# Moving the split weights and the transposed tokens of a hybrid decoder kernel by 16 and 32 bytes in SBUF

## The chip, the cores and the metric

The kernel runs on one core of a Trainium2 chip. The metric is the device time of one execution in microseconds (us); the kernel before takes 1882.4 us, the median of three runs (1880.84 to 1884.98).

## The reference

Two residual layers over 256 tokens of width 1024, and a final norm. Each layer has an attention mixer and then a product-key expert mixer (PEER). All of it is float32.

```
for i in range(2):
    h = rms_norm(x, attn_norm[i])
    x = x + (even_mixer if i == 0 else mla_mixer)(h, ...)      # projections, attention, out-projection
    h = rms_norm(x, ffn_norm[i])
    x = x + peer_ffn(h, w_q, sub_keys, u_tab, v_tab)
return rms_norm(x, final_norm)

# peer_ffn: q = h @ w_q; two top-16 lists of 128 keys for each of 8 heads; the best 16 of their sums name
# 16 of 16384 experts for each token and head; act = gelu(u_tab[expert] . h); out = sum softmax * act * v_tab[expert]
```

## The kernel before

The PEER mixer takes most of the time. The kernel doesn't gather experts. It multiplies all 256 tokens with the whole table `u` (16384 x 1024), multiplies the activations with a gate that is zero for every expert a token did not choose, and multiplies the result with the whole table `v`. Both tables stream through SBUF in units of 128 x 1024 float32 (512 KB), one DMA each on the sync queue, into three buffers `raw`.

TensorE takes its operands in fp32r, a rounded form of float32. To keep float32 precision each operand is split in two: `hi` is the rounded value and `lo` the rest. A product is then three matmuls: hi by hi, lo by hi, hi by lo. The class `Weights` (L46 on) splits each half unit of 512 columns: ScalarE writes `hi` from `raw` (L69), VectorE writes `lo` = raw - hi (L70). `hi` and `lo` have five buffers each (pools `hip` and `lop`). What the tokens need is split by `to_T` (L283 on): TensorE transposes a chunk of 128 features of all 256 tokens, ScalarE writes `hi[c]` (L290), VectorE `lo[c]` (L291). There are eight such chunks; `tiles8` (L281) reserves them.

A matmul has a *stationary* operand, 128 x 128, that a LDWEIGHTS puts into the array ahead of it, and a *moving* operand that is streamed through. The stages use the two kinds of tile in both roles:

- **projections** (`product`, L301 to L303) and **out-projection** (L438 to L440): tokens or head outputs stationary, split weights moving, 512 columns (352 and 200 in some).
- **PEER query and scores** ("the S stage", `split_prod`, L806 to L808): split weights stationary, tokens moving, 256 columns. One layer has 16 query blocks (tiles `rhi`, `rlo`) and 128 expert blocks (tiles `hi`, `lo`), 24 matmuls each. While the expert blocks run, the gates are made: groups of mostly eight bf16 matmuls (L990) stand between the S matmuls. In the query blocks and the first expert blocks VectorE also makes the top-16 lists (L831 to L838).
- **PEER output** ("the V stage", `mm`, L1078 to L1080): the split activations `ohA`, `ohB` stationary, the split weights moving, 512 columns, 1536 matmuls a layer.

Which byte of a partition an operand starts at is decided by its pool alone, which lays its tiles one behind another. Before, a `hi` or `lo` buffer of the weights is 2048 bytes a partition and a token tile is 1024 bytes, so all buffers of a kind start at the same place modulo 512 bytes.

Of the kernel before, what the change touches and what calls it, by code (L numbers as in the profile page):

```python
# [10 lines left out]
F32R = mybir.dt.float32r  # L11
# [9 lines left out]
S, D = 256, 1024  # L21
# [17 lines left out]
class Weights:  # L39
# [19 lines left out]
    def split(self, j):  # L59
        while self.n_split <= min(j, len(self.halves) - 1):  # L60
            k, s = self.halves[self.n_split]
            self.load(k + self.ahead)
            w = self.units[k][1]
            hi = self.hip.tile([128, 512], F32R, name="hi")
            self.tc_hp = self.tc.high_priority(offset=HP)
            self.tc_hp.__enter__()
            lo = self.lop.tile([128, 512], F32R, name="lo")
            src = self.raw[k][:, s * w:(s + 1) * w]
            self.nc.scalar.activation(hi[:, :w], src, AF.Copy)  # L69
            self.nc.vector.tensor_tensor(lo[:, :w], src, hi[:, :w].bitcast(F32), op=OP.subtract)  # L70
            self.tc_hp.__exit__(None, None, None)
            self.parts[self.n_split] = (hi, lo)
            self.n_split += 1
# [70 lines left out]
def body(tc, I, out):  # L144
    nc = tc.nc
    with ExitStack() as ctx:
# [132 lines left out]
            return x[tb][c // 4][:, c % 4 * 128:(c % 4 + 1) * 128]  # L279

        def tiles8(pool, name, dtype=F32R):  # L281
            return [pool.tile([128, S], dtype, name=f"{name}{c}") for c in range(8)]

        def to_T(src, c, col, hi, lo, psp, tag):

# [221 lines left out]
        def even_mixer(gcol):  # L507
            with ExitStack() as c1:
# [8 lines left out]
                va = ap.tile([128, 2, 64], F32, name="va")  # L517
                iw = ap.tile([128, 2, 8], F32, name="iw")
                oT = [tiles8(ap, f"oT{i}") for i in range(2)]
                selm = [ap.tile([128, 128 * (q + 1)], BF, name=f"selm{q}") for q in range(2)]  # L520
                hi, lo = tiles8(ap, "hi"), tiles8(ap, "lo")
                st = {}

# [104 lines left out]
        def mla_mixer(gcol):  # L628
            with ExitStack() as c1:
# [5 lines left out]
                cq = ap.tile([128, 2, D], F32, name="cq")  # L635
                scr = ap.tile([128, 2, D], F32, name="scr0")
                hi, lo = tiles8(ap, "hi"), tiles8(ap, "lo")
                chi, clo = tiles8(ap, "chi"), tiles8(ap, "clo")
                oT = [hi, lo]
# [520 lines left out]
```

## Time and profile before

| | |
|---|---|
| time, median of three runs | 1882.4 us |
| the profiled execution: its time, its span | 1880.96 us, 1879.2 us |
| busy: TensorE matmul, weight load, VectorE, ScalarE | 99%, 89%, 77%, 66% |
| chain of work that ended last, by engine | TensorE 92%, VectorE 6%, ScalarE 1%, issue 1% |
| the S stage's share of that chain (L806 to L808) | 39% |
| the V stage's share (L1078 to L1080) | 36% |

The span is the time from the first instruction to the last on the core; what lies around it is 1.8 us here. "Busy" of a matmul counts its streaming and its tail, so that two matmuls in a row overlap in the profile: how fast TensorE goes is read from the distance between starts, not from one matmul's duration. [...]

### The profile page before, as it was taken

To read this page: it belongs to the slowest core of one execution; us is meant where nothing else is said; L and a number is where in the kernel's file an instruction comes from. 1 tells how busy PE (TensorE), PEld (TensorE's weight loads), DVE (VectorE), ACT (ScalarE), POOL (GpSimd) and SP (SyncE) were. 2 spreads that over 40 slices of the span, in tenths; PEclk is the share of its full clock that TensorE was granted. 3 is DMA by queue.
4 is the path that set the end of the run, shared out by engine and by line. 5 is a ranking of instruction groups with operands and counts; after the bars stand their busy time and mean duration, and the time that the engine had idled before them with its cause. 6 is when DMAs were issued, how large, how long until landed. Compare 5 with 4: busy or idle time off the path is not lost.

```text
span 1879.2 us, 35739 instructions
## 1 busy us (share of the span) xinstructions
PE 1852.2 (99%) x12588; PEld 1664.2 (89%) x12588; DVE 1447.2 (77%) x3710; ACT 1247.3 (66%) x3060; POOL 6.4 (0%) x10
## 2 busy tenths in 40 slices
PE   8999999999999999999999999999999999999997
PEld 7769999999999888888888799999999988888886
DVE  7958998888898666666677699988888976666665
ACT  5646556888887555555576665688888865555554
POOL 0000000000000000000000000000000000000001
PEclk9989999999999999999999999999999999999999
DMA  6415565555555555556554345655555555555554
GB/s 191 134 46 170 163 197 182 168 169 174 165 170 179 191 193 193 191 193 192 188 162 136 122 139 190 190 174 165 172 167 169 171 189 191 192 192 193 192 193 136
DMA packets 90179, 323.33 MB, mean 172 GB/s; under 512 B 10512, under 2 KB 10896, under 8 KB 89744
## 3 DMA queue, kind: packets, MB, share of 16 engines
q1 hardware_dynamic: 88704, 318.71, 52.6%
q8 instruction: 99, 1.62, 0.3%
q0 software_dynamic: 288, 2.10, 0.3%
q14 instruction: 80, 0.66, 0.1%
q10 hardware_dynamic: 1008, 0.25, 0.1%
HBM read 319.97 MB, written 1.05 MB: 171 GB/s over the span
## 4 chain that ended last, share of the span: by engine, by line
PE 92%; DVE 6%; ACT 1%; issue 1%; DMA 0%; ACTq 0%; DVEq 0%
PE S L806 13%; PE S L807 13%; PE S L808 13%; PE acc L1079 12%; PE acc L1080 12%; PE acc L1078 12%; PE scp L990 3%; PE pj L301 2%; PE pj L303 2%; PE pj L302 2%; DVE lo L70 2%; PE bk L372 1%; DVE A L834 1%; DVE A L831 1%; DVE A L838 1%; PE pj L438 1%
## 5 line engine op out<-in xcount | busy, mean ns | idle before, releaser
L69 ACT ACTIVATE hi<-raw 128x512 fp32r<-128x512 f32 (+2 forms) x1214 | 756.0, 628 | 566.6 <-DVE lo L70 198.0
L70 DVE TENSOR_TENSOR lo<-raw,hi 128x512 fp32r<-128x512 f32 (+2 forms) x1214 | 826.2, 685 | 351.4 <-ACT hi L69 344.8
L806 PE MATMUL S<-hi,hi 128*128 128x256 f32 x2048 | 579.3, 283 | 1.8 <-ACT A L1019 1.8
L808 PE MATMUL S<-hi,lo 128*128 128x256 f32 x2048 | 568.9, 278 | 0.4
L807 PE MATMUL S<-lo,hi 128*128 128x256 f32 x2048 | 568.7, 278 | 0.0
L806 PEld LDWEIGHTS S<-hi,hi 128*128 128x128 f32 x2048 | 386.0, 188 | 2.6 <-ACT A L1019 2.6
L808 PEld LDWEIGHTS S<-hi,lo 128*128 128x128 f32 x2048 | 384.7, 188 | 1.2 <-DVE lo L70 1.1
L807 PEld LDWEIGHTS S<-lo,hi 128*128 128x128 f32 x2048 | 385.4, 188 | 0.0
L1079 PE MATMUL acc<-lo,ohB 128*128 128x512 f32 x512 | 201.2, 393 | 0.0
L1079 PE MATMUL acc<-lo,ohA 128*128 128x512 f32 x512 | 201.2, 393 | 0.0
L1080 PE MATMUL acc<-hi,ohA 128*128 128x512 f32 x512 | 199.9, 391 | 0.0
L1080 PE MATMUL acc<-hi,ohB 128*128 128x512 f32 x512 | 199.2, 391 | 0.0
L1078 PE MATMUL acc<-hi,ohA 128*128 128x512 f32 x512 | 159.2, 390 | 0.0
L1078 PE MATMUL acc<-hi,ohB 128*128 128x512 f32 x512 | 159.2, 390 | 0.0
L955 ACT ACTIVATE ohB<-ohB,RA 128x128 bf16<-128x128 bf16 x256 | 117.2, 525 | 0.0
L1078 PEld LDWEIGHTS acc<-hi,ohA 128*128 128x128 f32 x512 | 96.1, 188 | 22.0
L1078 PEld LDWEIGHTS acc<-hi,ohB 128*128 128x128 f32 x512 | 96.1, 188 | 21.9
L1079 PEld LDWEIGHTS acc<-lo,ohA 128*128 128x128 f32 x512 | 96.2, 188 | 20.8
L1079 PEld LDWEIGHTS acc<-lo,ohB 128*128 128x128 f32 x512 | 96.2, 188 | 20.7
L1080 PEld LDWEIGHTS acc<-hi,ohB 128*128 128x128 f32 x512 | 96.2, 188 | 20.3
L1080 PEld LDWEIGHTS acc<-hi,ohA 128*128 128x128 f32 x512 | 96.2, 188 | 20.3
L957 ACT ACTIVATE ohB<-iota,RA 128x128 bf16<-128x128 f32 x256 | 84.1, 435 | 0.0
(263 smaller groups left out, 2465.8 us busy)
## 6 DMA issues: line engine op xcount, KB each, us to landing
raw<-in_pu SPq DMA_DIRECT2D x256, 512.0 KB, 3.6
raw<-in_pv SPq DMA_DIRECT2D x256, 512.0 KB, 4.3
raw<-in_pq SPq DMA_DIRECT2D x32, 512.0 KB, 3.6
raw<-in_w SPq DMA_DIRECT2D x20, 512.0 KB, 3.7
raw<-in_uq SPq DMA_DIRECT2D x9, 512.0 KB, 4.0
raw<-in_w SPq DMA_DIRECT2D x12, 352.0 KB, 2.9
raw<-in_w0o SPq DMA_DIRECT2D x8, 512.0 KB, 3.6
raw<-in_w1o SPq DMA_DIRECT2D x8, 512.0 KB, 3.9
```

The costliest lines, as they stand in the source:

```text
L69: self.nc.scalar.activation(hi[:, :w], src, AF.Copy)
L70: self.nc.vector.tensor_tensor(lo[:, :w], src, hi[:, :w].bitcast(F32), op=OP.subtract)
L301: nc.tensor.matmul(ps[tb], hi[c][:, t], a, start=st, stop=False)
L806: nc.tensor.matmul(p, a, hi[c], start=first and i == 0, stop=False)
L807: nc.tensor.matmul(p, a, lo[c], start=False, stop=False)
L808: nc.tensor.matmul(p, b, hi[c], start=False, stop=last and i == 3)
L955: nc.scalar.activation(e[:, j // 2, :, j % 2], e[:, j // 2, :, j % 2], AF.Relu, bias=r[1], scale=r[2])
L957: nc.scalar.activation(e[:, j // 2, :, j % 2], iota, AF.Square, bias=r[0], scale=-1.0)
L990: nc.tensor.matmul(p[:, i], E[:, 1, i // 2, :, i % 2], G[:, s, i // 2, :, i % 2], start=i + s == 0, stop=True, skip_group_check=True)
L1078: nc.tensor.matmul(o, a[:, 0, t], w[0], start=b == 0, stop=False)
L1079: nc.tensor.matmul(o, a[:, 0, t], w[1], start=False, stop=False)
L1080: nc.tensor.matmul(o, a[:, 1, t], w[0], start=False, stop=b == NK - 1)
```

## The change

Three allocations change. A weight buffer is allocated with 520 columns and used with 512 (2080 bytes in place of 2048). A token tile is allocated with 264 columns and used with 256 (1056 bytes in place of 1024), and chunks 1, 3, 5, 7 start 4 columns (16 bytes) into their place. `tiles8` also reserves the head outputs `oT` of the first layer and the four sets of token tiles of each mixer.

```diff
-            hi = self.hip.tile([128, 512], F32R, name="hi")
+            hi = self.hip.tile([128, 520], F32R, name="hi")[:, :512]
...
-            lo = self.lop.tile([128, 512], F32R, name="lo")
+            lo = self.lop.tile([128, 520], F32R, name="lo")[:, :512]
...
         def tiles8(pool, name, dtype=F32R):
-            return [pool.tile([128, S], dtype, name=f"{name}{c}") for c in range(8)]
+            return [pool.tile([128, S + 8], dtype, name=f"{name}{c}")[:, 4 * (c % 2):4 * (c % 2) + S] for c in range(8)]
```

Every engine has the same instructions in the same order with the same waits in both programs; only addresses differ. The places of the operands in a partition, in bytes modulo 128 (the built programs' addresses; the buffers from first to last):

| operand | before | after |
|---|---|---|
| weights `hi`, five buffers | 96 96 96 96 96 | 96 0 32 64 96 |
| weights `lo`, five buffers | 96 96 96 96 96 | 0 32 64 96 0 |
| S stage: token tiles `hi` 0 to 7, and `lo` 0 to 7 | 32 (all) | 96 16 32 80 96 16 32 80 |
| V stage: `ohA`, `ohB` | 32 (all) | 96 (all) |
| first layer: token tiles of the projections, head outputs | 96 (all) | change like those of the S stage |
| `raw` | 96 (all) | 96 (all) |

The slices used within these tiles start at multiples of 512 bytes, except in the two projections with 200 and 352 columns.

## Rows read from the trace of the kernel before

**Rows 1.** The page: chain that ended last, by engine and by line.
```profile
PE 92%; DVE 6%; ACT 1%; issue 1%; DMA 0%; ACTq 0%; DVEq 0%
```

**Rows 2.** Busy time by stretch: us, then each engine's, granted clock, DMA share, GB/s.
```profile
150.00:280.00 130.00, 128.96 (x1101) 127.77 (x1100) 123.42 (x554) 80.13 (x162) 0.00 (x0) 1.00 0.54 177
280.00:596.00 316.00, 316.00 (x2974) 313.52 (x2973) 275.96 (x633) 259.12 (x773) 0.00 (x0) 1.00 0.53 171
620.00:940.00 320.00, 320.00 (x1400) 262.57 (x1399) 200.22 (x350) 182.92 (x349) 0.00 (x0) 1.00 0.59 191
1090.00:1185.00 95.00, 94.52 (x816) 93.85 (x815) 94.84 (x482) 54.99 (x110) 0.00 (x0) 1.00 0.52 167
1200.00:1516.00 316.00, 316.00 (x2975) 313.54 (x2974) 276.03 (x632) 259.04 (x773) 0.00 (x0) 1.00 0.54 172
1530.00:1850.00 320.00, 320.00 (x1400) 262.58 (x1399) 200.21 (x350) 183.23 (x350) 0.00 (x0) 1.00 0.59 191
```

**Rows 3.** Timeline of TensorE, V stage: start us, us, engine line op.
```profile
799.85 0.39 PE L1079 MATMUL acc<-lo,ohB 128*128 128x512 f32 x1
800.08 0.39 PE L1080 MATMUL acc<-hi,ohB 128*128 128x512 f32 x1
...
803.97 0.39 PE L1079 MATMUL acc<-lo,ohA 128*128 128x512 f32 x1
```

**Rows 4.** Timeline of TensorE, first layer's out-projection.
```profile
138.36 1.07 PE L438 MATMUL pj<-hi,oT 128*128 128x512 f32 x4
...
141.08 1.07 PE L438 MATMUL pj<-hi,oT 128*128 128x512 f32 x4
```

**Rows 5.** Timeline of TensorE, first layer's projections, around a group of transposes.
```profile
42.66 0.39 PE L301 MATMUL pj<-hi,hi 128*128 128x512 f32 x1
...
43.79 0.39 PE L303 MATMUL pj<-hi,lo 128*128 128x512 f32 x1
44.11 0.71 PE L572 MATMUL bk<-kkT,iqT 64*128 64x128 f32 x8
...
45.09 0.39 PE L302 MATMUL pj<-lo,hi 128*128 128x512 f32 x1
...
46.02 0.40 PE L303 MATMUL pj<-hi,lo 128*128 128x512 f32 x1
```

**Rows 6.** Timeline of TensorE, S stage, one place.
```profile
412.57 0.28 PE L808 MATMUL S<-hi,lo 128*128 128x256 f32 x1
...
415.29 0.28 PE L808 MATMUL S<-hi,lo 128*128 128x256 f32 x1
```

**Rows 7.** Timeline of TensorE, S stage, another place.
```profile
512.78 0.28 PE L806 MATMUL S<-hi,hi 128*128 128x256 f32 x1
...
514.90 0.28 PE L806 MATMUL S<-hi,hi 128*128 128x256 f32 x1
```

**Rows 8.** L807 by line (count, busy us, mean ns) in 405:460, 484:520, 280:596.
```profile
L807 PE MATMUL S<-lo,hi 128*128 128x256 f32 x142 | 39.3, 277 | 0.0
...
L807 PE MATMUL S<-lo,hi 128*128 128x256 f32 x90 | 25.4, 282 | 0.0
...
L807 PE MATMUL S<-lo,hi 128*128 128x256 f32 x818 | 227.2, 278 | 0.0
```

**Rows 9.** Timeline of TensorE, 200-column projections at two places.
```profile
17.86 0.25 PE L301 MATMUL pj<-hi,hi 128*128 128x200 f32 x1
17.95 0.28 PE L302 MATMUL pj<-lo,hi 128*128 128x200 f32 x1
...
22.84 0.26 PE L301 MATMUL pj<-hi,hi 128*128 128x200 f32 x1
22.93 0.28 PE L302 MATMUL pj<-lo,hi 128*128 128x200 f32 x1
```

**Rows 10.** VectorE's L70 by line in 150:280 (count, busy us, mean ns | idle).
```profile
L70 DVE TENSOR_TENSOR lo<-raw,hi 128x512 fp32r<-128x512 f32 x83 | 57.1, 694 | 4.1 <-ACT hi L69 2.6 <-PE S L808 1.0
```

## The prediction

> **What bounds the kernel now.** I read the chain of waits first: 92% of it is TensorE [rows 1]. [...] The query blocks (150 to 280 us, and 1090 to 1185) are different: there VectorE is busy for 123.4 of 130 and 94.8 of 95 us, so what TensorE saves there it mostly loses again in waiting. The change alters no instruction and no wait. [...]
>
> **What the distances say.** In the V stage 18 matmuls take 803.97 - 799.85 = 4.12 us, 228.9 ns each [rows 3]. In the first layer's out-projection, same shape, same clock, 12 take 141.08 - 138.36 = 2.72 us, 226.7 ns each [rows 4]. Matmul, width and type are the same; what I can find that differs is the operands' place. While one matmul streams, the next one's weights are loaded (weight loads are busy for 313.5 of 316 and 262.6 of 320 us, all beside matmuls [rows 2]), so the pair that meets is the moving operand and the next stationary one. Their distance modulo 128 bytes is 64 in the V stage and 0 in that out-projection. In the S stage, distance 64 throughout, two paces exist: 24 matmuls in 2.72 us, 113.3 ns each [rows 6], and 18 in 2.12 us, 117.8 ns [rows 7]. The slow pace lasts for many blocks and then goes. Place alone doesn't decide either: in the first layer's projections, distance 0, five intervals take 1.13 us (226 ns) ahead of a group of transposes, and four take 0.93 us (232 ns) behind it [rows 5]. [...] Distance and phase together decide, and a constant distance lets a good or a bad phase persist. That is inferred, not shown.
>
> **The change part by part.** *V stage.* The five weight buffers stand at 0, 32, 64, 96 and 96 or 0 modulo 128 and the activations at 96, so the distance is 64 for one buffer in five, and 0, 32 or 96 for the others. Before, the excess is 228.9 - 226.7 = 2.2 ns on each of 2 x 1536 matmuls, 6.8 us. If only distance 64 pays it, four fifths go: -5.4 us. Distances 32 and 96 stand in no row; from below they are bounded by the 226.7 ns of rows 4 (-6.8 us), from above by the 232 ns of rows 5 (+3.1 ns each, +9.5 us). [...]
>
> *S stage.* How much of it is slow: L807 lasts 277 ns in a fast stretch, 282 in a slow one and 278 over the whole [rows 8], about one in four after rounding. The stretch 280 to 596 us has some 2455 S matmuls (2974 less 512 gate matmuls and a few), so the slow pace costs 2455 x 0.25 x 4.5 ns = 2.8 us, 5.5 us in both layers. After the change the distances take all eight multiples of 16 evenly, and from chunk to chunk they alternate, so no distance lasts. Bounds: all fast, -5.5 us; all slow, 4910 x 0.75 x 4.5 ns = +16.6 us. Of the eight distances one is 64 and one is 0, the two seen with a slow pace, so less than before should be slow, but each switch of distance may cost something while the streams fall into step. I take half of the excess away: -2.7 us.
>
> *Query blocks.* VectorE holds them back, and its L70 (83 of 694 ns here [rows 10]) is the one instruction there whose operands move against each other (`raw` at 96, `hi` at 0 to 96). 83 and some 60 in the second layer, by 10 ns either way, is 1.4 us either way; I take 0. TensorE's savings are hidden there.
>
> *Projections and out-projections.* 588 matmuls of 512 columns by the plans, at either pace 2 to 5 ns apart: at most 3 us, both signs; 0. *The padding itself* costs no instruction and no transfer, and `raw`, where the DMAs land, keeps its place; VectorE's and ScalarE's splits elsewhere stand beside matmuls that are busy all the time, and a split later by 10 ns is covered by the idle time that L70 has ahead of it.
>
> Sum: -5.4 - 2.7 = -8.1 us; the profiled execution goes from 1880.96 to 1872.9. It lay 1.4 us below the median of the runs, so the median goes from 1882.4 to 1874.3, say 1874 us.
>
> [...] The rows show one shape at 226.7 and 228.9 ns [rows 3, 4] and at 113.3 and 117.8 ns [rows 6, 7]. [...]
>
> **The rivals.**
>
> *No change.* The paces come from the phase at which the streams start, set by what interrupts them, and the places are irrelevant. For it: rows 5 show both paces at one distance, and in the S stage both at one distance. Against: the V stage's pace is the same in all of rows 3 and differs from rows 4. Then V stays at 228.9, S keeps its quarter: 1882 us, within 0.2%.
>
> *Slower: no phase can last.* With one distance throughout, three quarters of the S stage run at 113.3 ns, and those are the streams in step. If every change of distance throws them out of step, and chunks now alternate by odd multiples of 16, the S stage runs at the pace of rows 7 everywhere, +16.6 us, and the V stage, where buffers change each fourth to sixth matmul, gains nothing: 1899 us. With the 232 ns of rows 5 in V as well, +9.5, it is 1908. It decides against me as soon as its loss passes V's gain: 5.4 us / 4.5 ns = 1200 more slow S matmuls, a slow share of half in place of a quarter. Against it: a group of gate matmuls interrupts the S stage every 5 us and mostly leaves the pace as it was, so the streams fall into step quickly. [...]
>
> [...]
>
> **How the numbers follow.** The forecast (-3.8 to -14 us) 0.46; no change 0.23; slower 0.26; the floor falls 0.05. The last counts as faster, as does the forecast: faster by over 0.2% 0.51, within 0.2% (about what a measurement of this kernel can tell from no change) 0.23, slower 0.26. The forecast's own range is 1868 to 1879. For 8 in 10, the range reaches to 1863 (all S and V excess gone, 12.3 us, and the query blocks and projections with it, some 6 us more) and to 1894, about two thirds of the way to the slow rival.
>
> **What would show it.** Right: V's starts 226.7 to 227.3 ns apart, with slower matmuls only around one buffer in five; S nearer 113.3 than 114.5; the counts of rows 2 for equal stretches go up. Wrong: V at 229 or more, or S matmuls that take turns by chunk between two distances with a mean above 115 ns. If the time moves and these distances don't, the cause lies outside TensorE, in VectorE's L70 and the query blocks.

## The result and the profile after

The changed kernel takes 1913.7 us, the median of four runs (1911.01 to 1915.41), against 1882.4 us: a ratio of 1.0164, 95% interval 1.0146 to 1.0181. It is slower by 31 us, where 1874 was forecast and the range ended at 1894. The profiled execution has a span of 1911.9 us against 1879.2.

Where the 32.7 us went is read from one line of each stage: the first and last start (us) of L807 mark the S stage of a layer, those of L1078 on `ohB` the V stage (whose last matmuls, on `ohA`, start some 4 us later in both kernels). Before:

```profile
L807 PE MATMUL S<-lo,hi x1024: 276/276/364, 206.0 to 595.5; 128*128 128x256 f32 x171
L1078 PE MATMUL acc<-hi,ohB x256: 388/392/394, 595.7 to 943.4; 128*128 128x512 f32 x128
L807 PE MATMUL S<-lo,hi x1024: 276/276/364, 1126.7 to 1516.2; 128*128 128x256 f32 x171
L1078 PE MATMUL acc<-hi,ohB x256: 388/392/394, 1516.5 to 1864.1; 128*128 128x512 f32 x128
```

After (the three durations are the shortest, median and longest in ns):

```profile
L807 PE MATMUL S<-lo,hi x1024: 274/281/364, 208.9 to 607.3; 128*128 128x256 f32 x171
L1078 PE MATMUL acc<-hi,ohB x256: 388/394/401, 607.5 to 960.2; 128*128 128x512 f32 x128
L807 PE MATMUL S<-lo,hi x1024: 274/280/370, 1146.4 to 1544.9; 128*128 128x256 f32 x171
L1078 PE MATMUL acc<-hi,ohB x256: 388/392/398, 1545.1 to 1896.9; 128*128 128x512 f32 x128
```

The S stages grew from 389.5 to 398.4 and 398.5 us (17.9 us together), the V stages from 347.7 and 347.6 to 352.7 and 351.8 (9.2 us). The remaining 5.6 us lie ahead of the S stages, in the mixers and the query blocks. The busy time of the same stretches as in [rows 2] shows it as fewer matmuls, in windows that lie inside one stage in both kernels:

```profile
280.00:596.00 316.00, 316.00 (x2895) 313.21 (x2895) 270.25 (x615) 252.05 (x751) 0.00 (x0) 1.00 0.53 167
620.00:940.00 320.00, 320.00 (x1379) 258.54 (x1378) 197.33 (x346) 180.51 (x345) 0.00 (x0) 1.00 0.59 189
1200.00:1516.00 316.00, 315.72 (x2875) 312.85 (x2875) 270.53 (x626) 250.51 (x733) 0.00 (x0) 1.00 0.53 169
```

TensorE is still busy for all of it but 0.3 us, at granted clock 1.00 (the full one) as before; it has done 2895 matmuls where it did 2974, and 1379 for 1400. So each takes longer; next to nothing of the loss is waiting. In the chain TensorE's share rises from 92 to 97% and VectorE's falls from 6 to 1% [rows 1]; ScalarE's `hi` (L69) waits 81.3 us in all for VectorE's `lo` (L70), where it waited 198.0:

```profile
PE 97%; DVE 1%; ACT 1%; DMA 0%; issue 0%; ACTq 0%; DVEq 0%
```

The timeline at the places of [rows 3] and [rows 6] gives the pace. In the V stage 15 matmuls take 803.71 - 800.24 = 3.47 us, 231.3 ns each:

```profile
800.24 0.39 PE L1079 MATMUL acc<-lo,ohA 128*128 128x512 f32 x1
800.47 0.39 PE L1080 MATMUL acc<-hi,ohA 128*128 128x512 f32 x1
...
803.71 0.40 PE L1080 MATMUL acc<-hi,ohB 128*128 128x512 f32 x1
```

In the S stage, where before 24 matmuls ran at 113.3 ns, 19 now take 2.24 us, 117.9 ns each:

```profile
413.45 0.28 PE L808 MATMUL S<-hi,lo 128*128 128x256 f32 x1
413.57 0.28 PE L806 MATMUL S<-hi,hi 128*128 128x256 f32 x1
...
415.69 0.28 PE L806 MATMUL S<-hi,hi 128*128 128x256 f32 x1
```

Below, "S" and "V" are the mean distance between the starts of neighbouring matmuls of a stage, over the whole trace (pairs with a gate group between them, and query blocks, left out): before 114.6 and 228.9 ns, after 118.1 and 231.9. Where single distances are given to the ns, they come from the same start times in the trace; the lines shown here round to 10 ns.

### The profile page after: what moved, and what is told of

The parts are those of the page before. It is cut to its first block, busy times and chain, and to the rows that moved or that the text cites. A ratio compares the mean times of both kernels' runs of the same rounds, so it can differ in the third digit from the quotient of the medians.

```text
span 1911.9 us, 35739 instructions
## 1 busy us (share of the span) xinstructions
PE 1886.4 (99%) x12588; PEld 1687.2 (88%) x12588; DVE 1449.8 (76%) x3710; ACT 1249.3 (65%) x3060; POOL 6.4 (0%) x10
## 4 chain that ended last, share of the span: by engine, by line
PE 97%; DVE 1%; ACT 1%; DMA 0%; issue 0%; ACTq 0%; DVEq 0%
PE S L806 14%; PE S L807 14%; PE S L808 14%; PE acc L1079 12%; PE acc L1078 12%; PE acc L1080 12%; PE scp L990 3%; PE pj L301 2%; PE pj L303 2%; PE pj L302 2%; PE bk L372 1%; PE scp L1027 1%; PE pj L438 1%; PE pj L439 1%; PE pj L440 1%; PE bk L413 1%
## 5 line engine op out<-in xcount | busy, mean ns | idle before, releaser
L69 ACT ACTIVATE hi<-raw 128x512 fp32r<-128x512 f32 (+2 forms) x1214 | 756.6, 628 | 591.9 <-PE acc L1080 232.9
L70 DVE TENSOR_TENSOR lo<-raw,hi 128x512 fp32r<-128x512 f32 (+2 forms) x1214 | 826.1, 685 | 373.4 <-ACT hi L69 366.1
L807 PE MATMUL S<-lo,hi 128*128 128x256 f32 x2048 | 575.2, 281 | 0.0
L808 PE MATMUL S<-hi,lo 128*128 128x256 f32 x2048 | 574.9, 281 | 0.0
L807 PEld LDWEIGHTS S<-lo,hi 128*128 128x128 f32 x2048 | 385.8, 188 | 0.0
L1078 PE MATMUL acc<-hi,ohB 128*128 128x512 f32 x512 | 161.1, 394 | 0.0
L1078 PE MATMUL acc<-hi,ohA 128*128 128x512 f32 x512 | 161.1, 394 | 0.0
L1078 PEld LDWEIGHTS acc<-hi,ohA 128*128 128x128 f32 x512 | 96.1, 188 | 22.8
L1078 PEld LDWEIGHTS acc<-hi,ohB 128*128 128x128 f32 x512 | 96.1, 188 | 22.8
```

What stands on the lines that cost most here:

```text
L807: nc.tensor.matmul(p, a, lo[c], start=False, stop=False)
L808: nc.tensor.matmul(p, b, hi[c], start=False, stop=last and i == 3)
L1078: nc.tensor.matmul(o, a[:, 0, t], w[0], start=b == 0, stop=False)
```

## The experiments

Twelve kernels were run. All have the same instructions in the same order with the same waits as the kernel before; only places in SBUF differ. "Distance" is the start of the next stationary operand less that of the moving one, modulo 128 bytes where nothing else is said; the places are those of the built programs. The first expectations speak of 96 for both stages in e4; with that sign it is 96 in the V stage and 32 in the S stage.

| run | S ns | V ns | us | ratio, 95% interval |
|---|---|---|---|---|
| before | 114.6 | 228.9 | 1882.4 | |
| after | 118.1 | 231.9 | 1913.7 | 1.0164, 1.0146 to 1.0181 |
| e1 weights alone | 118.1 | 231.9 | 1912.4 | 1.0157, 1.0140 to 1.0174 |
| e2 tokens alone | 117.5 | 228.9 | 1901.1 | 1.0094, 1.0077 to 1.0111 |
| e3 all behind the weights 64 bytes later | 119.9 | 226.7 | 1910.1 | 1.0143, 1.0126 to 1.0160 |
| e4 the same, 32 bytes | 118.2 | 233.3 | 1917.8 | 1.0183, 1.0166 to 1.0200 |
| e5 gates and V's stationary tiles 64 bytes later | 117.1 | 226.7 | 1890.5 | 1.0037, 1.0024 to 1.0051 |
| e6 weight buffers at 96 and 32 in turn | 116.9 | 231.2 | 1905.1 | one run |
| e7 other constant distances | 117.3, 117.8 | 230.2, 233.3 | 1908.3 | one run |
| e8 distances of 16 and 48 | 118.4, 118.5 | 233.2, 231.7 | 1914.0 | one run |
| e9 V's stationary tiles alone | 114.5 | 226.7 | 1876.8 | 0.9968, 0.9957 to 0.9979 |
| e10 gates alone | 117.0 | 233.3 | 1908.4 | one run |
| e11 two distances in turn, modulo 512 | 118.8 | 231.1 | 1915.3 | one run |
| e12 as e9, gates 448 bytes later | 114.5 | 226.7 | 1874.4 | one run |

(Two figures: first and second layer.)

**e1 and e2: each half of the change alone.** e1 keeps the first two lines of the change, e2 the third.

```diff
e1  -hi = self.hip.tile([128, 512], F32R, name="hi")
    +hi = self.hip.tile([128, 520], F32R, name="hi")[:, :512]      # and lo
e2  -return [pool.tile([128, S], dtype, ...) for c in range(8)]
    +return [pool.tile([128, S + 8], dtype, ...)[:, 4 * (c % 2):4 * (c % 2) + S] for c in range(8)]
```

> Only the weight buffers are spaced by 2080 bytes; the token tiles keep their spacing of 1024. In-step theory (a distance that stays lets the two reads of TensorE keep step, every change of it costs): the V stage meets a new buffer every few matmuls as in the changed kernel and goes from 228.9 to about 232 ns a matmul (+9 us); the S stage's distance changes only with the buffer, each 12 matmuls, so it lies between 114.6 and 118.5 ns (0 to +20 us): 1892 to 1905 us. Distance theory (each distance has its own price, 0 and 64 modulo 128 cheap, the others dear): the V stage the same 232, the S stage the mean over four distances, about 117: 1902 us or more.

> Only the token tiles are spaced by 1056 bytes with the odd ones 16 bytes in; the weights as before. V stage at 228.9 ns by both theories, since no token tile is in it. In-step theory: the S stage changes distance with each chunk, every third matmul, and slows as in the changed kernel to about 118.5 ns: +18 to +22 us, 1901 us. Distance theory: the S stage has four distances, two of them odd multiples of 16; about 117 to 119 ns, 1895 to 1903 us.

The new weight buffers make the whole loss, in both stages; the tokens alone make most of the S stage's (117.5 ns) and leave V alone at 228.9, as they must. The two don't add up: once the weight buffers stand at four different places, the tokens' spacing makes no further difference (118.1 and 231.9 ns in e1 as in the change). "Weights alone" needs a caution: ten buffers longer by 32 bytes push everything behind them by 320 bytes, in e1 as in the change, so the tokens, the `ohA` and `ohB` tiles and the gates' operands stand elsewhere too (64 bytes on, modulo 128). e1's 1912.4 us fits the distance theory's "1902 or more" and lies above the in-step theory's 1905; but that theory's own terms, +9 and up to +20 us, reach 1911, and both allow e2's 1901. So these two don't decide between them.

**e3 and e4: one distance throughout, another one.** A pad behind the weight pools moves everything behind them.

```diff
 small = ctx.enter_context(tc.tile_pool(name="small", bufs=2))
+ctx.enter_context(tc.tile_pool(name="padp", bufs=1)).tile([128, 16], F32, name="pad")   # e4: [128, 8]
```

> As before the change, but everything allocated behind the weight buffers stands 64 bytes later: distance 0 modulo 128 in the S and V stage, 64 in the first layer's mixer, constant in each. In-step theory: V falls to 226.7 ns (-7 us), S keeps one of its two paces for long stretches, about 114.5: 1872 to 1880 us. Distance theory: V 226.7, S near 113.3 throughout: 1869 us. If places don't matter: 1882 us with V at 228.9.

> As before the change, but everything allocated behind the weight buffers stands 32 bytes later: distance 96 modulo 128 in the S and V stage, constant. This tells the theories apart. In-step theory: a constant distance keeps step; V at or below 229 ns and all alike, S mostly near 113.3: 1870 to 1886 us. Distance theory: 96 is one of the dear distances; V about 232 ns, S about 118: 1908 us or more.

This is the pair that decides on the in-step theory, against it. With distance 0 the V stage runs at its best pace, 11 matmuls from 799.84 us to 802.34 us in 2.50 us, 227 ns each:

```profile
799.84 0.39 PE L1079 MATMUL acc<-lo,ohB 128*128 128x512 f32 x1
...
802.34 0.39 PE L1080 MATMUL acc<-hi,ohA 128*128 128x512 f32 x1
```

and its S stage at 120 ns from beginning to end (14 matmuls from 413.30 to 414.98 us), slower than either pace before:

```profile
413.30 0.28 PE L807 MATMUL S<-lo,hi 128*128 128x256 f32 x1
413.42 0.28 PE L808 MATMUL S<-hi,lo 128*128 128x256 f32 x1
...
414.98 0.28 PE L806 MATMUL S<-hi,hi 128*128 128x256 f32 x1
```

In e4 no distance ever changes either, and V takes 233.3 ns; 11 matmuls in 802.45 - 799.88 = 2.57 us:

```profile
799.88 0.40 PE L1079 MATMUL acc<-lo,ohB 128*128 128x512 f32 x1
...
802.45 0.39 PE L1080 MATMUL acc<-hi,ohA 128*128 128x512 f32 x1
```

So a constant distance is no guarantee of a good pace: each that was run had its price, and the order of the prices is not the same in both stages. Distance 0 was best in V (226.7 ns, against 228.9 at 64 and 233.3 at 96) and worst in S (119.9, against 118.2 at 32 and 114.6 at 64). The gates' operands moved along in both runs; e10 below shows that this alone can slow S to 117.0, but not to the 120 ns that e3 keeps throughout. The distance theory's 113.3 ns for S in e3 was as wrong as the in-step theory's 114.5.

**e5: V's tiles alone, as it was meant.** Distance 0 in V, and 64 in S as before.

```diff
+c1.enter_context(tc.tile_pool(name="padp", bufs=1)).tile([128, 16], F32, name="pad")
 ohp = c1.enter_context(tc.tile_pool(name="ohp", bufs=2))
...
 rawpool = rawc.enter_context(tc.tile_pool(name="rawt", bufs=1))
+rawpool.tile([128, 112], F32, name="rpad")     # the query blocks' tiles stay where they were, modulo 512
```

> As before the change, with the V stage's stationary tiles (and nothing else that a matmul of the S or V stage reads) 64 bytes later: distance (stationary minus moving, modulo 128) 64 in the S stage as before, 0 in the V stage. Price theory (each constant distance has its own price in each stage: V 226.7 ns at 0, 228.9 at 64, 233.3 at 96; S 119.9 at 0, 114.6 at 64, 118.2 at 32): V at 226.7, S unchanged at 114.6, 3072 x 2.2 ns = 6.8 us less, 1875.6 us. If the stages influence each other or the modulus is not 128: S other than 114.6 or V other than 226.7.

V did as expected. S did not: no operand of its matmuls had changed its place modulo 512 bytes, and it went from 114.6 to 117.1 ns, by spending most of its time at the pace of 117.8 in place of 113.3. What had moved beside V's tiles are the gate tiles, which share their buffers. e9 and e10 take the two apart.

**e6, e7, e8: changing distances, other distances.** e6 spaces the weight buffers by 2112 bytes; e7 and e8 give each layer its own constant offset of the S stage's tokens and of the `ohA`, `ohB` tiles (and of the gates' operands, which lie in these), in places that are 128 bytes longer.

```diff
e6  -hi = self.hip.tile([128, 512], F32R, name="hi")
    +hi = self.hip.tile([128, 528], F32R, name="hi")[:, :512]      # and lo, and two pads that keep the rest in place modulo 128
e7  +hp.tile([128, S + 32], F32R, name=f"{n}{c}")[:, (0, 24)[layer]:][:, :S]        # e8: (12, 4)
    +ohp.tile([128, 544], F32, name=n)[:, (16, 24)[layer]:][:, :512]...             # ohA and ohB; e8: (20, 28)
```

> Token and activation tiles as before; the five weight buffers of a kind alternate between 96 and 32 bytes modulo 128, so that every matmul is at distance 64 or 0 but the distance changes with the buffer. If only the distance of the pair in hand has a price, the V stage is the mean of 228.9 and 226.7 weighted 3 to 2, 228.0 ns, and the S stage that of 114.6 and 119.9, 116.8 ns. If changes of distance cost by themselves, both lie above: V at 230 ns or more, S at 118 or more.

> Weights as before; tokens of the S stage and stationary tiles of the V stage moved by a constant in each layer, with tiles spaced by 128 bytes more (a multiple of 128). First layer: S at distance 64, V at 0, as controls: 114.6 and 226.7 ns if the modulus is 128; other values if 256 or 512 counts, since the extra spacing changes these. Second layer: S at 96, V at 32, not seen before; price theory gives no number, only that S lies in 113.3 to 120 and V in 226.7 to 234.

> The same construction with quarter steps: first layer S and V at distance 16, second layer S and V at 48. [...]

The controls of e7 failed, and that is its result. S's control isn't a clean one, since the gates' operands moved with it by 64 bytes, as in e5. V's is: at distance 0 modulo 128, but with tiles spaced by 128 bytes more, V takes 230.2 ns in place of 226.7. Its timeline shows how that mean comes about. Each `ohA` or `ohB` tile serves 12 matmuls; of five tiles in a row, here the first start on each, the first takes 743.47 - 740.75 = 2.72 us (227 ns a matmul), the next two 2.79 and 2.80 us (233), and the fourth 2.73 (228):

```profile
740.75 0.61 PE L1078 MATMUL acc<-hi,ohA 128*128 128x512 f32 x2
...
743.47 0.64 PE L1078 MATMUL acc<-hi,ohB 128*128 128x512 f32 x2
...
746.26 0.63 PE L1078 MATMUL acc<-hi,ohA 128*128 128x512 f32 x2
...
749.06 0.62 PE L1078 MATMUL acc<-hi,ohB 128*128 128x512 f32 x2
...
751.79 0.62 PE L1078 MATMUL acc<-hi,ohA 128*128 128x512 f32 x2
```

Modulo 512 the distances of these tiles are 256, 128, 384, 0 and 256. So 0 and 256 get the best pace (228 and 227 ns), 128 and 384 don't (both 233): 128 bytes, which the prediction had taken for the whole period, is not; in V 256 fits, and a new pace sets in within some three matmuls of a change of tile. Read the same way, e7's second layer prices distance 32 (32, 160, 288 and 416 modulo 512): 233.3 ns on all four tiles, as dear as the 96 of e4. e8's V takes about 233 ns on all tiles at distance 16 and on two of the four at 48, 230.0 on the other two; the layer means are 233.2 and 231.7. In S the distances of e6, e7 and e8 change every few matmuls, so they don't price one distance by itself; e6's S (116.9) came out at the price theory's 116.8, its V (231.2) above the 228.0. Every mixture tried is slower than before.

**e9 and e10: the gates and V apart.** A buffer of `ohA` or `ohB` is 2560 bytes (a multiple of 512) and the two uses take different parts of it.

```diff
 tiles():   -ohp.tile([128, 4, 128], F32, name=n)...
            +ohp.tile([128, 640], F32, name=n)[:, g:g + 512]...     # gates: e9 g = 0, e10 g = 16, e12 g = 112
 wsplit():  -ohp.tile([128, 4, 128], F32, name=...)...
            +ohp.tile([128, 640], F32, name=...)[:, v:v + 512]...   # V stage: e9 v = 16, e10 v = 0, e12 v = 16
```

> In e5 the stationary tiles of the V stage were moved by 64 bytes, and with them the gate tiles that lie in the same buffers; V fell to its floor, but the S stage, none of whose operands had moved, went from 114.6 to 117.1 ns. Here only the V stage's use of these buffers is moved by 64 bytes; the gates keep their place. If the gates' place set which of its two paces the S stage runs at, S is back at 114.6 ns, V at 226.7: 1875.6 us, faster than both kernels. If any other effect of the move did (chance, the writes of VectorE and ScalarE in the V stage), S stays near 117: 1890 us.

> The counterpart: only the gate tiles are moved by 64 bytes, the V stage's use of the buffers keeps its place. If the gates' place sets the S stage's pace: S at about 117.1 ns as in e5, V at 228.9: 1897 us. If not: S at 114.6, 1882 us.

Both came out by the first theory in S: 114.5 ns with the gates where they were, 117.0 with the gates 64 bytes on. So in these runs the place of the gates' operands set the pace at which the S matmuls ran behind a group of gate matmuls. Whether the gate matmuls' reads do that, or the writes of VectorE and ScalarE into the same tiles, no run separates. It is not chance either: before the change S has a slow stretch from 484 to 520 us [rows 8], and the same stretch of the second layer, 920.7 us later, is slow again (L807, 1404.7 to 1440.7 us):

```profile
L807 PE MATMUL S<-lo,hi 128*128 128x256 f32 x89 | 25.1, 282 | 0.0
```

e9 is faster than both kernels: 1876.8 us, 0.9968 of before. Its V stage is at its best pace, 10 matmuls from 800.05 to 802.32 us in 2.27 us, 227 ns each:

```profile
800.05 0.39 PE L1079 MATMUL acc<-lo,ohA 128*128 128x512 f32 x1
...
802.32 0.39 PE L1078 MATMUL acc<-hi,ohB 128*128 128x512 f32 x1
```

e10 had a surprise. Its V stage has every operand at the same place modulo 512 as before, where it ran at 228.9 ns; here it runs at 233.3 throughout. The seam between the stages shows when it starts. Before, S comes in at 114 ns (8 matmuls from 594.66 to 595.57 us) and V runs at 229 (7 from 595.68 to 597.28):

```profile
594.66 0.28 PE L806 MATMUL S<-hi,hi 128*128 128x256 f32 x1
...
595.57 0.28 PE L808 MATMUL S<-hi,lo 128*128 128x256 f32 x1
595.68 0.39 PE L1078 MATMUL acc<-hi,ohB 128*128 128x512 f32 x1
...
597.28 0.39 PE L1079 MATMUL acc<-lo,ohB 128*128 128x512 f32 x1
```

In e10 it comes in at 118 (11 from 601.50 to 602.80) and V runs at 234 from its first matmul on (8 from 602.92 to 604.79):

```profile
601.50 0.28 PE L806 MATMUL S<-hi,hi 128*128 128x256 f32 x1
...
602.80 0.28 PE L808 MATMUL S<-hi,lo 128*128 128x256 f32 x1
602.92 0.40 PE L1078 MATMUL acc<-hi,ohB 128*128 128x512 f32 x1
...
604.79 0.40 PE L1080 MATMUL acc<-hi,ohB 128*128 128x512 f32 x1
```

That would fit a phase which the S stage hands on. But e2, with the same V places modulo 512 and the spacing of before, also comes in slowly, at 117 ns (9 from 606.30 to 607.35), and its V soon runs at 229 (11 from 608.62 to 611.14):

```profile
606.30 0.28 PE L808 MATMUL S<-hi,lo 128*128 128x256 f32 x1
...
607.35 0.28 PE L808 MATMUL S<-hi,lo 128*128 128x256 f32 x1
...
608.62 0.39 PE L1079 MATMUL acc<-lo,ohB 128*128 128x512 f32 x1
...
611.14 0.62 PE L1080 MATMUL acc<-hi,ohA 128*128 128x512 f32 x2
```

So S's pace at the seam does not settle V's. Start by start the two V paces look different: 226, 229, 232 ns over and over before and in e2, an even 233 to 234 in e10. Each sets in within five matmuls, in both layers, and lasts to the end of the stage. The buffers' spacing of 2560 in place of 2048 bytes is another difference of e10. Its pattern is the same on all four buffers, where e7's follows the buffer, which speaks against the spacing; e9 and e12 have it too and keep 226.7. What picks the pattern stays open.

**e11: changes of distance, modulo 512.**

```diff
-hi = self.hip.tile([128, 512], F32R, name="hi")
+hi = self.hip.tile([128, 640], F32R, name="hi")[:, 112 * (self.n_split % 2):][:, :512]      # and lo
```

> Weight buffers use alternately their first byte and byte 448 of a place that is 2560 bytes long, so that modulo 512 (and not only 128, as in e6) every matmul has one of two distances whose constant prices are known: V 228.9 and 226.7, S 114.6 and 119.9. The distance changes with each half unit, that is every 6 matmuls in V and every 12 in S. If a change costs nothing: V 227.8, S 117.3 ns. If changes cost by themselves: V at 230 to 232 as in the changed kernel.

V takes 231.1 ns. Had each distance its price of before, the mean would be 227.8; had distance 64 the dearer pace that e10 showed, (226.7 + 233.3) / 2 = 230.0. It lies above both, so in V a change of distance seems to cost something by itself, 1.1 to 3.3 ns a matmul when buffers alternate (if addresses modulo 512 are all that counts; the weight buffers are spaced by 2560 bytes here too). Half unit by half unit the starts lie 230.7 and 231.5 ns apart on average: neither of the two distances gets the 226.7 ns that 0 gets when it stays. In S the 118.8 ns is the mean of 117.8 and 119.9, the slower pace of distance 64 and that of distance 0: there no cost of the change itself is needed to explain it.

**e12: the gates the other way.**

> V stage's tiles moved by 64 bytes as in e9, gate tiles by 448 bytes, that is 64 the other way. V at 226.7 ns. For S no theory here gives a number; if the gates' place sets its pace it may be anything between 113.3 throughout (1869 us) and 117.8 throughout (1893 us).

S stays at 114.5, V at 226.7: 1874.4 us in one run, beside e9's 1874.1 to 1879.4. It is no better than e9 as far as one run tells. The equal mean of S hides another course: the slow stretches behind gate groups are gone (L807 at 486.7 to 522.7 us takes 278 ns, where the same stretch took 282 before [rows 8]), but the first two distances from start to start behind an interruption are 122.6 and 118.5 ns on average, where before they were 118.5 and 114.7:

```profile
L807 PE MATMUL S<-lo,hi 128*128 128x256 f32 x92 | 25.6, 278 | 0.0
```

## Why the prediction was wrong

*What bounds the kernel* was right: TensorE is busy throughout the four S and V stretches [rows 2], and in V a matmul that takes 3.0 ns longer makes, 3072 times, the 9.2 us by which the two stages grew. So there each nanosecond of a matmul counts fully. That places matter was right too, though the unit was not: it counted distances modulo 128 bytes, and e7 shows V at two paces, 227 and 233 ns, at one distance modulo 128. One shape at one granted clock, 1.00, took 226.7 (e3), 228.9 (before), 231.9 (after) and 233.3 ns (e4, e10) by the place of its operands alone, or by what ran before it. By which way the place acts is not shown.

*The V stage* (-5.4 us forecast, +9.2 measured) is the step that failed first. The prediction had 226.7 ns for distance 0 and 228.9 for 64, no row for 32 and 96, bounded them by 226.7 and 232, and its sum took the lower end, for which no row spoke. e4 put V at a distance of 96 throughout and e7's second layer at 32, and both measured 233.3: above the upper end. A second fault is the period: of the pairs that the change puts at distance 0 modulo 128, two fifths stand at 128 modulo 256, which took 233 in e7. These prices nearly make the loss: by the built programs' places a fifth of the changed kernel's V pairs stand at 0 modulo 256, and 226.7 ns for these and 233.3 for all others make 232.0, where 231.9 was measured. That is an estimate, not a proof: distances 64 and 96 modulo 256 stood still in no run, and the fault that each distance was given a price whatever came before remains, since in e11 the buffers take turns and run above the mean of their prices. The gain that was there, 2.2 ns a matmul, was real: e9 collects it with one distance, and measures 5.8 us of the 6.8 that the term had as its most.

*The S stage* (-2.7 us forecast, +17.9 measured) failed on the same ground: it took the distances that no row showed for mostly fast, which was the author's estimate. Constant ones measured 119.9 (0, e3) and 118.2 (32, e4), both above the 117.8 that the term had as its dearest pace. The quarter at 117.8 ns was read as a loss that mixing would dilute; the stage as a whole was already near the best it has been seen at: about three quarters of it ran at 113.3, and of the variants only e9 and e12 come to its mean of 114.6. The prediction also had no term for the gates' operands, which the change moves by 320 bytes; a move by 64 cost S 2.4 ns a matmul in e10, and how much of the changed kernel's S is theirs no run separates. Of the rival "no phase can last" the S part, +16.6 us, came true nearly to the number, and its account for both stages, 1908 us, is the nearest to 1913.7. But that streams get out of step is not shown, and the agreement is in part luck: constant distances ran just as slowly (S at 119.9 ns in e3, 118.2 in e4, 118.1 after the change), so it isn't the turn-taking alone.

*Query blocks and projections* (0 forecast) hold 5.6 us, which were not divided further.

*The chance of 0.05 that the floor falls* stands for a 512-column pace below 226.7 ns, and no run shows one: close to half of V's matmuls have moving operands at a multiple of 64 bytes in the changed kernel, and no two starts there lie less than 224 ns apart; their mean is 231.9.

*The range* ended 14 us short of the slow rival. Both V's upper bound and the S bound stood in the text and made 1908; the range should have reached there, since the choice between the ends rested on no row.

Open: what makes the paces. Shown is that they depend on the operands' place (V at 226.7 ns in e3 and e9, 233.3 in e4), on more than the address modulo 128 (227 and 233 ns in e7), and on the place of the gates' tiles, which are used in between (S at 114.5 ns in e9, 117.0 in e10). Which places give which pace was not found beyond those that were run.

## What to carry to other kernels

Where TensorE is busy all the time, read the distance between starts, stage by stage, before and after any change that moves a tile: here 1.6% lay there, with 0.3 us of idle time in 952 us to show for it. Tiles that stood at equal places modulo 512 bytes were not bad as such (228.9 ns in V before, 226.7 in e9); spreading them replaced one known pace by a mixture that was worse in every case tried here, 1901 to 1915 us against 1882. Move one operand of one stage, keep all others at their place modulo 512 bytes, and measure both stages, since a buffer shared with another stage takes that one along, as in e5 (S from 114.6 to 117.1 ns).

## What the runs showed of the hardware that was not expected

- A 512-column fp32r matmul that loads new weights each time took 226.7 ns at best as a steady pace at granted clock 1.00, in all runs here; a 256-column one 113.3 at best. Single distances go down to 224 ns, with longer ones beside them. Starting close to half of the moving buffers at a multiple of 64 bytes (e1 and the change) did not lower this floor; no run has them all there.
- In e5 and e10 the S stage, none of whose operands had changed its place modulo 512 bytes, ran 2.2 and 2.1% slower (117.1 and 117.0 for 114.6 ns), because the gates' tiles, read by the matmuls that stand between its own, had moved by 64 bytes.
- The V stage kept one pace over 350 us: 233.3 ns in e10 and 228.9 before with operands at the same places modulo 512. The 228.9 is the mean of single distances of 226, 229 and 232 ns that repeat, the 233.3 is even; each sets in within five matmuls and comes out the same in both layers.
